# Two pools of SBUF tiles trade places: the stationary tiles of the feed-forward products move from the far end of the partition to its middle

## Chip, cores and metric

One NeuronCore of one Trainium2 chip runs the whole kernel. The metric is device time in microseconds, the median of three runs. TensorE (PE) does the matrix products, VectorE (DVE), ScalarE (ACT) and GpSimd (POOL) the rest, and SyncE (SP) issues the transfers.

## What is computed

One decoder block over 2048 positions of 1024 channels, after 16 learned positions: a normalisation, an input projection, a mixer of two head groups, an output projection with a residual, then the part that the change touches, a gated feed-forward block, and a last normalisation:

```python
n2 = rmsnorm(h, norm2_g[i])
ff = jax.nn.silu(n2 @ w_gate[i]) * (n2 @ w_up[i])      # 1024 x 2816 each
h = h + ff @ w_down[i]                                 # 2816 x 1024
out = rmsnorm(h, final_norm_g)[:, N_META:]
```

## The kernel before

**Products.** A float32 product is made of three fast matmuls (`mm3`, lines 115 to 119): each operand is split into a high part and a low remainder, and high x high, high x low, low x high are summed in PSUM. Each of the three loads a stationary operand of 128 x 128 and streams a moving operand of 128 x 512. `split` casts the high part on ACT (line 110) and takes the remainder on DVE (line 85).

**Feed-forward.** The 2048 positions are two halves `b` of 1024. Gate and up products use a seven-product scheme on 2 x 2 blocks (`seven`): the normalised rows stand as seven moving operands `X["b11"]`, `"b21"`, `"t2"`, `"t3"`, `"t1"`, `"t4"`, `"b22"`, each a high and a low tile of 8 KB per partition; the weights come in 512 KB loads (`load_raw`), are combined on POOL (`s1`, `s2`, `s4`), and are split by `part` into the rotating stationary tiles `wch` and `wcl` (ten slots each, 2 KB per partition and slot). One call of `seven` is 7 products of 12 matmuls, named `pr` in the trace; there are 44 calls. The usual order of the moving operands is b11, b21, t2, t3, t1, t4, b22; the very first call (`early`) does b11, b21, t1, b22, t2, t3, t4. The down products (`dmm`, named `pd`) do the same with the roles turned: split pieces of `ff` (`fh`, `fl`) are stationary, in the slots of `wch` and `wcl`, and the split weights are the moving tiles, in the places of b11, b21, t2 and t3 (named db11, db21, dt2, dt3).

**Where tiles lie.** A pool opened with `side="right"` is put directly below the one before it, counted from the far end of the partition (at 224 KB), and tiles within a pool go up in the order in which they are first named. From the sizes, in KB from the start of the partition:

| tiles | pool | from | to |
|---|---|---|---|
| b11, b21, b22, t1 (high and low each) | `xa`, left | 21.7 | 85.7 |
| raw loads | `xa`, left | 85.7 | 101.7 |
| t2, t3, t4 (high and low each) | `xb`, right | 102 | 150 |
| s1, s2, s4, gate and up results, u | `wc`, right | 150 | 184 |
| `wch`, then `wcl` | `wc`, right | 184 | 224 |

The output projection before it, in the trace `po`, has its own tiles in the same space, in pools that are closed when the feed-forward pools open: `wb` (160 to 224, the split weights `wh`, `wl`, moving), `mc` (154 to 160), `xu1` (138 to 154), `wraw` (130 to 138, the rows `hx` that are stored as `h2_d`), `wo` (102 to 130, with the stationary `mh`, `ml` at 104 to 120 and the scratch `jk`). The `xa` tiles begin at a multiple of 64 bytes; all tiles on the right begin 32 bytes past one.

**Order.** Instructions are put in order per engine when the program is built, by a simulated timeline, and wait for each other through semaphores. The first writer of a pool that lies over closed pools waits for the last users in those pools: in the instructions of this program the first cast into `wch` waits for the last `po` matmul, and the first cast into `xt2h` for the last two stores of `hx`, although its own place lies over `pin` and `mh` alone.

Of the kernel before, what the change touches and what calls it, by code (L numbers as in the profile page):

```python
# [10 lines left out]
F32R = mybir.dt.float32r  # L11
# [5 lines left out]
P = 128  # L17
# [20 lines left out]
def kernel(  # L38
# [68 lines left out]
    def split(hi, lo, src, scale=None, e=V):  # L107

        if scale is None:
            A.copy(hi, src)  # L110
            tt(lo, src, hi.bitcast(F32), S_, e)
        else:
            A.activation(hi, src, AF.Copy, scale=scale)
            stt(lo, src, scale, hi.bitcast(F32), M_, S_)
# [731 lines left out]
    gu = ExitStack()  # L846
# [87 lines left out]
            x_rows(0, t - 2, ("b11", "b21", "b22", "t1"))  # L934
    wo.close()
    wb_s.close()
    wc_p = gu.enter_context(tc.tile_pool(name="wc", bufs=1, side="right"))
    xb_p = gu.enter_context(tc.tile_pool(name="xb", bufs=1, side="right"))

    def load_raw(w, f):  # L940
        raw = xa_p.tile([P, KD, P], F32, name="raw", tag="raw", bufs=4)
# [1 line left out]
        return raw  # L943

    def part(src):
        hi = wc_p.tile([P, 4, P], F32R, name="wch", tag="wch", bufs=10)
        lo = wc_p.tile([P, 4, P], F32R, name="wcl", tag="wcl", bufs=10)
        split(hi, lo, src)
        return hi, lo

# [11 lines left out]
    def seven(ws, c, done, early=False):  # L962
# [3 lines left out]
        def prod(a, xn):  # L966
            o = mm_tile("pr")
            ah, al = a if isinstance(a, tuple) else part(a)
            for k in range(4):
                mm3(o, ah[:, k], al[:, k], X[xn][0][:, k], X[xn][1][:, k], k == 0, k == 3)  # L970
            return o
# [26 lines left out]
    def parts(ws):  # L998
        return [part(a) for a in ws]
# [93 lines left out]
    def f_split(g):  # L1093
        if g >= len(seq):
            return
        raw = fraw.pop(g)
        ffs[g] = []
        for q in range(NQ):
            n = min(4, NM - 4 * q)
            hi = wc_p.tile([P, 4, P], F32R, name="fh", tag="wch", bufs=10)  # L1100
            lo = wc_p.tile([P, 4, P], F32R, name="fl", tag="wcl", bufs=10)
            split(hi[:, :n], lo[:, :n], raw[:, 4 * q:4 * q + n])
            ffs[g].append((hi, lo))

# [82 lines left out]
    w_load(0, 2)  # L1187
    w_split(0, 0)
    f_split(0)
    w_split(0, 1)  # L1190
    f_split(1)
    w_split(0, 2)
    f_load(2)
    g = 0
    for g, (i, n) in enumerate(seq):
        if g == 0:
            o, o1 = mm_tile("pd"), mm_tile("pd")
            for m in range(NM + 4):
                if m < NM:
                    dmm(o, 0, m)  # L1200
                if m >= 4:
                    dmm(o1, 1, m - 4)
        elif g == 1:
            o = o1
        else:
            o = mm_tile("pd")
            for m in range(NM):
                dmm(o, g, m)
        ffs.pop(g)
        if g >= 1:  # L1210
            f_split(g + 1)
        f_load(g + 3)
        if n == 3:
            w_load(i + 1, 0)
            w_split(i + 1, 0)
        if n == 5:
            w_load(i + 1, 1)
            w_load(i + 1, 2)
        take(i, n, o)
        if n == len(pairs) - 1:  # L1220
            w_split(i + 1, 1)
            w_split(i + 1, 2)
# [32 lines left out]
```

## Time and profile before

| | |
|---|---|
| median of 3 runs | 1885.26 us (1885.22 to 1886.34) |
| profiled execution, its own time | 1885.98 us |
| span of its instructions | 1884.2 us, mean granted clock 0.988 |
| PE busy | 1822.9 us, 97% |
| DVE, ACT, POOL busy | 1232.4, 673.8, 816.9 us |
| feed-forward (`pr`), about | 578 to 1459 us |
| down products (`pd`), about | 1459 to 1877 us |

The profiled execution took 1.8 us more than its span, and 0.7 us more than the median of the runs. A matmul's recorded duration is modelled and overlaps the next one; the distance from one start to the next is what a matmul costs. Times in the rows are microseconds from the start of the span, durations of groups in nanoseconds.

### The profile page before, as it was taken

How to read it: one execution, taken by the hardware profiler on the slowest of the kernel's cores; microseconds unless marked ns; L12 is line 12 of the kernel's file. 1: busy time of each engine (PE TensorE's matmuls, PEld its weight loads, DVE VectorE, ACT ScalarE, POOL GpSimd, SP SyncE). 2: the span in 40 equal slices, each digit the busy share in tenths (PEclk: the TensorE clock that was granted, in tenths of full speed). 3: DMA queues.
4: the chain of work that ended last, by engine and by line, in shares of the span. 5: the costliest groups of instructions: out<-in, count | busy, mean ns of one | idle time of the engine just before them, and what ended most of it. 6: DMA issues, size and time to landing. Idle time of an engine off the chain costs nothing.

```text
span 1884.2 us, 23676 instructions
## 1 busy us (share of the span) xinstructions
PE 1822.9 (97%) x8497; PEld 1495.4 (79%) x8497; DVE 1232.4 (65%) x1913; ACT 673.8 (36%) x1213; POOL 816.9 (43%) x619
## 2 busy tenths in 40 slices
PE   7989997899999999999999999999999999999998
PEld 5767786788887888888887788888888888888886
DVE  6996777866457866656667866766666444445763
ACT  4333334243454333332334332333223343333441
POOL 1684425633344565453656866665662000003400
PEclk9999998999999999999999999999999999999999
DMA  6255424444355344443436554554447765536771
GB/s 182 72 176 183 144 96 145 174 168 140 112 175 167 106 157 140 140 157 107 156 117 211 194 166 151 163 179 150 133 150 228 227 198 170 154 109 208 245 218 69
DMA packets 260518, 298.37 MB, mean 158 GB/s; under 512 B 17148, under 2 KB 204048, under 8 KB 255536
## 3 DMA queue, kind: packets, MB, share of 16 engines
q1 hardware_dynamic: 260304, 296.84, 49.5%
q8 instruction: 67, 1.10, 0.2%
q14 instruction: 51, 0.42, 0.1%
q0 software_dynamic: 96, 0.01, 0.0%
HBM read 202.37 MB, written 96.53 MB: 159 GB/s over the span
## 4 chain that ended last, share of the span: by engine, by line
PE 73%; DVE 3%; DMA 2%; POOL 1%; issue 1%; ACT 1%; DVEq 0%; POOLq 0%; ACTq 0%
PE pr L117 14%; PE pr L118 14%; PE pr L119 14%; PE pd L117 8%; PE pd L118 8%; PE pd L119 8%; PE po L117 2%; PE po L119 2%; PE po L118 2%; DVE wcl L85 1%; PE pgate L774 1%; DMA hr<-h_d 1%; PE ptx L865 1%; DMA xp<-xr_d 0%; PE ppool L760 0%
## 5 line engine op out<-in xcount | busy, mean ns | idle before, releaser
L110 ACT CAST wch<-raw 128x512 fp32r<-128x512 f32 x176 | 108.7, 621 | 268.2 <-PE pr L118 240.8
L85 DVE TENSOR_TENSOR wcl<-raw,wch 128x512 fp32r<-128x512 f32 x176 | 175.7, 1001 | 37.4 <-ACT wch L110 37.0
L85 DVE TENSOR_TENSOR fl<-fr,fh 128x512 fp32r<-128x512 f32 x168 | 116.9, 707 | 126.3 <-ACT fh L110 126.2
L110 ACT CAST fh<-fr 128x512 fp32r<-128x512 f32 x168 | 96.2, 584 | 202.4 <-PE pd L118 175.0
L110 ACT CAST wch<-s 128x512 fp32r<-128x512 f32 x132 | 82.1, 622 | 224.2 <-PE pr L118 174.6
L85 POOL TENSOR_TENSOR s<-raw 128x512 f32<-128x512 f32 x44 | 67.8, 1540 | 174.7 <-DVE wcl L85 75.3
L85 DVE TENSOR_TENSOR wcl<-s,wch 128x512 fp32r<-128x512 f32 x132 | 118.3, 896 | 19.4 <-ACT wch L110 19.1
L85 POOL TENSOR_TENSOR db22h<-db22h,hd 128x512 f32<-128x512 f32 x4 | 5.2, 1292 | 256.2 <-DVE db22h L85 256.2
L117 PE MATMUL pj<-wh,xh 128*128 128x512 f32 x256 | 102.6, 409 | 2.6 <-ACT xh L110 2.3
L117 PE MATMUL po<-wh,mh 128*128 128x512 f32 x256 | 103.8, 406 | 0.7 <-ACT mh L110 0.7
L119 PE MATMUL pj<-wh,xl 128*128 128x512 f32 x256 | 103.0, 407 | 0.0
L118 PE MATMUL pj<-wl,xh 128*128 128x512 f32 x256 | 102.7, 403 | 0.0
L119 PE MATMUL po<-wh,ml 128*128 128x512 f32 x256 | 100.4, 393 | 0.8 <-DVE ml L85 0.8
L118 PE MATMUL po<-wl,mh 128*128 128x512 f32 x256 | 100.7, 393 | 0.0
L85 POOL TENSOR_TENSOR rs<-rv,mhalf 128x1 f32<-128x1 f32 (+2 forms) x35 | 31.5, 900 | 154.1 <-DVE rv L91 144.8
L85 POOL TENSOR_TENSOR wr<-wr 128x512 f32<-128x512 f32 x44 | 66.8, 1519 | 72.4 <-DMA wr<-in_w_down_dram 64.5
L85 DVE TENSOR_TENSOR gt<-gt,ut 128x512 f32<-128x512 f32 x88 | 92.9, 1057 | 0.0
L85 POOL TENSOR_TENSOR tmp<-z,pk 64x512 f32<-64x512 f32 x32 | 50.8, 1588 | 79.8 <-issue 64.7
L85 DVE TENSOR_TENSOR gt<-pr,gt 128x512 f32<-128x512 f32 x66 | 45.5, 690 | 60.3 <-PE pr L119 60.1
L85 POOL TENSOR_TENSOR ut<-gt 128x512 f32<-128x512 f32 x22 | 33.6, 1528 | 107.2 <-DVE gt L85 107.2
L117 PE MATMUL pr<-xt2h,wch 128*128 128x512 f32 x176 | 70.5, 400 | 5.3 <-DVE gt L85 3.6
L1006 ACT ACTIVATE gt<-gt 128x512 f32<-128x512 f32 x88 | 55.6, 633 | 50.8 <-DVE gt L85 50.8
(392 smaller groups left out, 5586.1 us busy)
## 6 DMA issues: line engine op xcount, KB each, us to landing
fr<-ff_d SPq DMA_DIRECT2D x56, 704.0 KB, 4.9
raw<-in_w_gate_dram SPq DMA_DIRECT2D x44, 512.0 KB, 4.8
raw<-in_w_up_dram SPq DMA_DIRECT2D x44, 512.0 KB, 4.3
ff_d<-gt SPq DMA_DIRECT2D x22, 1024.0 KB, 3.9
pk<-pk_d SPq DMA_DIRECT2D x16, 1284.0 KB, 6.2
ff_d<-ut SPq DMA_DIRECT2D x22, 768.0 KB, 5.6
wr<-in_w_down_dram SPq DMA_DIRECT2D x22, 512.0 KB, 3.3
wd_d<-wr SPq DMA_DIRECT2D x22, 512.0 KB, 3.4
```

The costliest lines, as they stand in the source:

```text
L85: e.tensor_tensor(o, a, b, op=op)
L110: A.copy(hi, src)
L117: PE.matmul(o, lh, rh, start=first, stop=False)
L118: PE.matmul(o, lh, rl, start=False, stop=False)
L119: PE.matmul(o, ll, rh, start=False, stop=last)
L774: PE.matmul(pg[:, k * P:(k + 1) * P], glubd[:, k], gt[:, k], start=True, stop=True)
L865: PE.transpose(pt[:, k], r[:, (4 * h + k) * P:(4 * h + k + 1) * P], ident)
L1006: lambda i, j: A.activation(gt[:, i, j], gt[:, i, j], AF.Silu), b == 0 and f0 == 0)
```

## The change

The pool `xb` (t2, t3, t4 and their namesakes of the down products) is opened first and so lies at the far end. The pool `wc` follows, without the rotating stationary tiles, and these have a pool `wk` of their own, opened last. The number of slots and the order of all calls stay.

```diff
     wo.close()
     wb_s.close()
+    xb_p = gu.enter_context(tc.tile_pool(name="xb", bufs=1, side="right"))
     wc_p = gu.enter_context(tc.tile_pool(name="wc", bufs=1, side="right"))
-    xb_p = gu.enter_context(tc.tile_pool(name="xb", bufs=1, side="right"))
+    wk_p = gu.enter_context(tc.tile_pool(name="wk", bufs=10, side="right"))
...
     def part(src):
-        hi = wc_p.tile([P, 4, P], F32R, name="wch", tag="wch", bufs=10)
-        lo = wc_p.tile([P, 4, P], F32R, name="wcl", tag="wcl", bufs=10)
+        hi = wk_p.tile([P, 4, P], F32R, name="wch", tag="wch")
+        lo = wk_p.tile([P, 4, P], F32R, name="wcl", tag="wcl")
...
-            hi = wc_p.tile([P, 4, P], F32R, name="fh", tag="wch", bufs=10)
-            lo = wc_p.tile([P, 4, P], F32R, name="fl", tag="wcl", bufs=10)
+            hi = wk_p.tile([P, 4, P], F32R, name="fh", tag="wch")
+            lo = wk_p.tile([P, 4, P], F32R, name="fl", tag="wcl")
```

From the sizes, the places after it: `wch` at 102 to 122 KB, `wcl` at 122 to 142, the rest of `wc` at 142 to 176, t2, t3 and t4 at 176 to 224. The `xa` tiles stay. Every shift is a multiple of 2 KB.

## Rows read from the trace of the kernel before

**Rows 1.** Busy time by stretch: stretch, length, PE, PEld, DVE, ACT, POOL, clock, DMA.
```profile
650.00:1000.00 350.00, 350.00 (x1551) 285.43 (x1550) 231.28 (x296) 117.87 (x198) 184.34 (x125) 1.00 0.44 141
1060.00:1450.00 390.00, 390.00 (x1689) 317.00 (x1688) 269.90 (x330) 125.45 (x203) 236.21 (x155) 1.00 0.52 164
1470.00:1870.00 400.00, 400.00 (x1737) 325.85 (x1736) 208.40 (x308) 143.02 (x256) 43.36 (x38) 1.00 0.59 180
```
**Rows 2.** Waits of PE from 600 to 1880 us: total us, times, longest.
```profile
PE pr L117 <- DVE gt L85: 4.1, 3, 2.2
```
**Rows 3.** Groups of PE by form: out<-moving,stationary, count, busy us, mean ns.
```profile
L117 PE MATMUL pr<-xb21h,wch 128*128 128x512 f32 x176 | 69.7, 396 | 0.0
L117 PE MATMUL pr<-xt3h,wch 128*128 128x512 f32 x176 | 68.6, 390 | 0.0
...
L117 PE MATMUL pr<-xt4h,wch 128*128 128x512 f32 x176 | 69.0, 392 | 0.4 <-DVE gt L85 0.4
L117 PE MATMUL pd<-db11h,fh 128*128 128x512 f32 x176 | 69.7, 396 | 0.0
...
L117 PE MATMUL pd<-db21h,fh 128*128 128x512 f32 x144 | 57.0, 396 | 0.0
L117 PE MATMUL pd<-dt3h,fh 128*128 128x512 f32 x152 | 59.2, 390 | 0.0
L117 PE MATMUL pd<-dt2h,fh 128*128 128x512 f32 x144 | 56.3, 391 | 0.0
```
**Rows 4.** Timeline of PE, the first matmul of four successive products.
```profile
802.86 0.40 PE L117 MATMUL pr<-xb21h,wch 128*128 128x512 f32 x1
...
805.66 0.39 PE L117 MATMUL pr<-xt2h,wch 128*128 128x512 f32 x1
...
808.40 0.39 PE L117 MATMUL pr<-xt3h,wch 128*128 128x512 f32 x1
...
811.12 0.40 PE L117 MATMUL pr<-xt1h,wch 128*128 128x512 f32 x1
```
**Rows 5.** Timeline of PE, output projection: first and last of eleven matmuls in a row.
```profile
450.95 0.39 PE L117 MATMUL po<-wh,mh 128*128 128x512 f32 x1
...
453.22 0.39 PE L118 MATMUL po<-wl,mh 128*128 128x512 f32 x1
```
**Rows 6.** Timeline of ACT at the start of the feed-forward part.
```profile
577.24 1.14 ACT L110 CAST wch<-raw 128x512 fp32r<-128x512 f32 x2 [1.16 <-PE po L119]
...
580.84 0.62 ACT L110 CAST xt2h<-xp 128x512 fp32r<-128x512 f32 x1 [1.32 <-DMA h_d<-hx]
...
591.38 0.61 ACT L110 CAST xt3h<-xp 128x512 fp32r<-128x512 f32 x1
```
**Rows 7.** Timeline of PE in the same stretch, first matmuls of products and the last `po`.
```profile
576.81 0.39 PE L119 MATMUL po<-wh,ml 128*128 128x512 f32 x1
577.91 0.50 PE L117 MATMUL pr<-xb11h,wch 128*128 128x512 f32 x1 [0.71 <-ACT wch L110]
...
591.52 0.50 PE L117 MATMUL pr<-xt2h,wch 128*128 128x512 f32 x1 [1.36 <-ACT xt2h L110]
...
599.16 0.39 PE L117 MATMUL pr<-xt4h,wch 128*128 128x512 f32 x1
```
**Rows 8.** Tile hx from 574 to 582 us: its last store, its landing time, its waiter.
```profile
L817 SPq DMA_DIRECT2D h_d<-hx x1: 320/320/320, 578.0 to 578.0; - x1
...
  ACT xt2h L110: 1.3, 1
...
DMA to landing us min/median/max: 2.7/2.7/2.7
```
**Rows 9.** Timeline of DVE, the same stretch.
```profile
592.28 0.68 DVE L85 TENSOR_TENSOR xt3l<-xp,xt3h 128x512 fp32r<-128x512 f32 x1
```
**Rows 10.** Busy time by stretch, columns as in rows 1: gaps of PE and the clock.
```profile
209.80:213.60 3.80, 0.47 (x3) 0.03 (x1) 3.71 (x8) 1.21 (x3) 2.99 (x2) 1.00 0.39 103
...
214.40:217.80 3.40, 3.40 (x14) 2.92 (x13) 3.31 (x10) 0.59 (x1) 0.86 (x1) 0.51 0.00 0
...
593.40:596.80 3.40, 3.40 (x9) 2.63 (x9) 1.53 (x4) 1.18 (x2) 0.00 (x0) 0.50 0.92 266
```

## The prediction

> **What bounds the kernel now.** I first looked where PE is idle, since the change touches only PE's operands. In three long stretches, 1140 us in all, PE is busy for the whole length, at full clock, with DVE at 52 to 69% and the others lower [rows 1]; from 600 us to the end PE waits only 4.1 us for others [rows 2]. So from 600 us on the time is a number of matmuls times the distance from one start to the next. That distance is not one number. In steady state the products on b21 take (805.66 - 802.86) / 12 = 233.3 ns each, those on t3 (811.12 - 808.40) / 12 = 226.7 ns, those on t2, which come after a slow product, (808.40 - 805.66) / 12 = 228.3 ns [rows 4]. The groups say the same in their modelled durations: 396 ns with a moving operand in b11 or b21 (t1 and b22 alike), in the down products too, 390 to 392 ns with one in t2, t3 or t4 [rows 3]. The slow ones are the tiles at 22 to 86 KB, the fast ones those on the right. So place, or something that goes with it, does cost time on this chip, 6.7 ns or 2.9% of a matmul, and the change is about place. The question is whose place.
>
> **Part 1, the rate of the products.** The change moves the stationary tiles from 184-224 KB to 102-142, and t2, t3, t4 from 102-150 to 176-224. The slow moving tiles stay at 22-86.
>
> For t2, t3, t4 the trace has nearly the new pair already: in the output projection the moving `wh`, `wl` lie at 160-224 and the stationary `mh`, `ml` at 104-120, and eleven matmuls in a row give (453.22 - 450.95) / 10 = 227 ns [rows 5]. That is the fast value, so I put nothing on these.
>
> For the slow tiles the new pair (moving at 22-86, stationary at 102-142) stands nowhere in the trace. The bounds: at best each comes down to 226.7 ns, at worst it stays at 233.3; worse than that no row shows for a matmul in steady state. Their number: b11, b21, t1, b22, three matmuls each, are 12 groups of 176 [one in rows 3], 2112; db11 is three groups of 176 and db21 three of 144 [rows 3], 960; together 3072. Times 6.67 ns that is 20.5 us. With no slow product ahead of them t2 and t4 (2 x 528 matmuls) would also lose their 1.67 ns, another 1.8 us. So part 1 is worth between 0 and -22.3 us.
>
> I take 0. The stationary tile's place leaves no mark in the trace: `wch` lies at 184-204 and `wcl` at 204-224, and the three matmuls of a triple, two with the one and one with the other, take the same; stationary at 184-224 with t3 and stationary at 104-120 with `wh` give the same 227 ns [rows 4, 5]. The nearness of the two isn't it either: t1 ends at 86 KB, 98 below the nearest stationary tile, and is slow; t2 begins at 102 KB, up to 122 below the farthest, and is fast once settled. What does sort the rows is the moving tile alone, by its place (below 86 or above 102 KB) or by its start: the `xa` tiles start at a multiple of 64 bytes, everything on the right, stationary tiles too, 32 bytes past one. The change leaves both as they are, since the `xa` tiles stay and every shift is a multiple of 2 KB.
>
> A rule to weigh here: the Trainium skill (TensorE: Matmul & The Clock Gate, Part 2: What happens when you issue a matmul) has the next tile's weights read through a port of their own, which takes no bandwidth from the running matmul. By that rule the stationary tiles' place can't matter, and part 1 is 0 as well. The trace agrees that their place leaves no mark, but not that place is without effect: the page has no reason for 233.3 against 226.7 ns.
>
> **Part 2, the start of the feed-forward part.** Here a wait changes hands. Now `wc` lies over `wb`, `mc` and `xu1`, and its first cast goes as soon as the last `po` is done, at 577.24 us; PE starts `pr` at 577.91 [rows 6, 7]. `xb` lies over `wo`, `wraw` and part of `xu1`, and its first cast, `xt2h`, waits for the last store of `hx`, issued at 578.0, landed 2.7 us later, and starts at 580.84 [rows 6, 8]. After the change `wk` lies over `wo`, `wraw` and `xu1`, so the first cast into `wch` inherits that wait, while `xb` lies over `wb` alone and is free at 577.2. `s1`, `s2`, `s4` stay over `mc`, `wb` and `xu1` and keep their start.
>
> The first `pr` moves from 577.91 to 580.84 + (577.91 - 577.24) = 581.51, 3.6 us later. Behind the waiting cast ACT has its other casts, and if the built order leaves those of `xt2h` and `xt3h` behind it, they wait too; DVE's remainders follow either way, and the SP queue holds only loads that wait for these casts. PE is then without work for 4.7 us from 576.81. A gap of 3.8 us was followed by 3.4 us at half clock (0.51, which is 1.2 GHz) [rows 10], so I add 1.7 us for that.
>
> Against this stands a stall that the kernel already has. PE now reaches t2 early, waits, starts at 591.52 [rows 7], gets its pieces one by one until DVE's last `xt3l` at 592.28 + 0.68 = 592.96 [rows 9], and then runs 3.4 us at half clock [rows 10]; it begins t4 only at 599.16 [rows 7]. After the change the four products before t2 take 48 x 0.2333 = 11.2 us, plus 0.45 us that they lose on the first remainders, plus 1.7 for the clock: t2 starts at 581.51 + 13.35 = 594.9, when its pieces are there if they come no more than 1.9 us later than now. Then t2 and t3 take 24 x 0.228 = 5.5 us and t4 starts at 600.3, 1.2 us later than now. Without the half clock it would be 0.5 us earlier; without the cover it is rival 2. So part 2 costs +1.2 us, between -0.5 and +5.3.
>
> **The sum.** 1885.98 us is the profiled execution, 0.7 over the median; 1.8 of it lie around the span and don't change. 1885.98 + 0 + 1.2 = 1887.2 for that execution, 1886.5 against the median of 1885.26. Within 0.2% (3.8 us), about what a measurement of this kernel tells from no change, it is the same.
>
> **Rival 1, the stationary tile matters after all.** It may matter for low moving tiles only, where no row can show it: then 233.3 falls to 226.7 ns at best, and the time is 1886.5 - 22.3 = 1864.2, or something between. For it: the one placement like the new one, the output projection, is fast [rows 5], and the slow tiles are those that never met a stationary tile in the middle. Against it: nothing else in the rows moves with the stationary place. DVE has room for 1.2% more speed [rows 1].
>
> **Rival 2, the later start isn't covered.** The casts of the t2 and t3 pieces stand behind the waiting cast on ACT, and their loads behind them, so the pieces come 3.6 + 1.7 us later, as PE does, and the old stall is met again. Then the whole delay stays: 1885.3 + 5.3 = 1890.6. It decides from the point where the last `xt3l` ends later than about 594.9 us, now 592.96. For it: the casts at 591.38 come after a silu that needs PE's second product [rows 6]. Against it: with `xb` free at once, ACT can cast the first pieces while it has nothing else.
>
> **Rival 3, the fast tiles become slow.** If t2, t3, t4 at the far end fall to 233.3 ns, 9 x 176 + 3 x 152 + 3 x 144 = 2472 matmuls [one of each in rows 3] pay 6.67 ns, 16.5 us, less the 1.8 already paid: 1886.5 + 14.7 = 1901.2. Against it stand the rows of `po` [rows 5], in which only stationary places up to 120 KB occur.
>
> **How the numbers follow.** Forecast (rate unchanged, start covered): 0.60, 1886.5 us, on its own 1884 to 1889. Rival 1: 0.22. Rival 2: 0.13. Rival 3: 0.05. Faster by over 0.2% is rival 1, 0.22; within 0.2% is the forecast, 0.60; slower is rivals 2 and 3, 0.18. Rival 1 is too likely to be left out, so the range reaches to it and to rival 2: 1863 to 1891; rival 3 stays outside.
>
> **What would show it.** Right: in steady state 233.3 ns between starts on b11 and b21, 226.7 on t3; the first `wch` cast released by the store of `hx` at about 580.8; the first `pr` near 581.5; a stretch at half clock after it; t2 without a wait; t4 at about 600. Wrong: groups of `pr` on b11 or b21 below 396 ns (rival 1, then the down products on db11 too), t3 above 390 (rival 3), or a wait of PE for `xt2h` beyond 595 us (rival 2). That the build shifts other orders by some us is the rest of the risk.

## The result and the profile after

| | before | after |
|---|---|---|
| median | 1885.24 us, 4 runs (1883.08 to 1886.34) | 1898.42 us, 4 runs (1896.79 to 1899.44) |
| profiled execution, its own time | 1885.98 us | 1898.18 us |
| span, mean granted clock | 1884.2 us, 0.988 | 1896.4 us, 0.984 |

The changed kernel is slower: ratio 1.0071, interval 1.0053 to 1.0088. In a later series with more runs it was 1.0055, interval 1.0041 to 1.0069 (below, the changed kernel again). The forecast was 1886.5 us in a range of 1863 to 1891, so the time lies outside it, on the side that had a chance of 0.18.

**The rate of the products did not change.** The changed kernel's groups of PE by form (out<-moving,stationary, count, busy us, mean ns):

```profile
L117 PE MATMUL pr<-xb21h,wch 128*128 128x512 f32 x176 | 69.8, 397 | 0.0
L117 PE MATMUL pd<-db11h,fh 128*128 128x512 f32 x176 | 69.7, 396 | 0.0
L117 PE MATMUL pr<-xt4h,wch 128*128 128x512 f32 x176 | 69.1, 392 | 0.8 <-DVE gt L85 0.4 <-ACT wch L110 0.3
L117 PE MATMUL pr<-xt3h,wch 128*128 128x512 f32 x176 | 68.5, 389 | 0.0
```

These are the values of [rows 3] to 1 ns. The timeline of PE, first matmuls of four successive products, gives the distances:

```profile
816.27 0.40 PE L117 MATMUL pr<-xb21h,wch 128*128 128x512 f32 x1
...
819.07 0.39 PE L117 MATMUL pr<-xt2h,wch 128*128 128x512 f32 x1
...
821.82 0.39 PE L117 MATMUL pr<-xt3h,wch 128*128 128x512 f32 x1
...
824.54 0.40 PE L117 MATMUL pr<-xt1h,wch 128*128 128x512 f32 x1
```

b21 takes (819.07 - 816.27) / 12 = 233.3 ns from start to start, t2 229.2 (228.3 there), t3 226.7, as in [rows 4]; 0.01 us over twelve matmuls is 0.8 ns. In the long stretches PE is as full as in [rows 1], at full clock (stretch, length, PE, PEld, DVE, ACT, POOL, clock, DMA):

```profile
655.00:1005.00 350.00, 350.00 (x1550) 285.29 (x1549) 227.60 (x291) 117.97 (x199) 181.62 (x123) 1.00 0.42 135
...
1480.00:1880.00 400.00, 400.00 (x1737) 325.87 (x1736) 209.28 (x310) 144.38 (x259) 43.27 (x38) 1.00 0.60 182
```

**The time went at the start of the feed-forward part.** The timelines of ACT, PE and DVE there (start, length, operation, idle time before it and what ended it):

```profile
581.52 0.62 ACT L110 CAST xt2h<-xp 128x512 fp32r<-128x512 f32 x1 [1.16 <-PE po L119]
...
585.66 1.14 ACT L110 CAST wch<-raw 128x512 fp32r<-128x512 f32 x2 [1.34 <-DMA h_d<-hx]
```
```profile
581.10 0.39 PE L119 MATMUL po<-wh,ml 128*128 128x512 f32 x1
586.33 0.79 PE L117 MATMUL pr<-xb11h,wch 128*128 128x512 f32 x1 [4.85 <-ACT wch L110]
...
589.39 0.80 PE L119 MATMUL pr<-xb11h,wcl 128*128 128x512 f32 x1 [0.98 <-DVE wcl L85]
...
602.06 0.40 PE L117 MATMUL pr<-xt2h,wch 128*128 128x512 f32 x1
...
608.00 0.47 PE L117 MATMUL pr<-xt4h,wch 128*128 128x512 f32 x1 [0.34 <-ACT wch L110]
...
614.26 0.47 PE L117 MATMUL pr<-xb11h,wch 128*128 128x512 f32 x1 [3.25 <-DVE gt L85]
```
```profile
582.19 1.19 DVE L85 TENSOR_TENSOR xt2l<-xp,xt2h 128x512 fp32r<-128x512 f32 x1
...
586.66 1.77 DVE L85 TENSOR_TENSOR xt3l<-xp,xt3h 128x512 fp32r<-128x512 f32 x1
...
588.64 1.30 DVE L85 TENSOR_TENSOR wcl<-raw,wch 128x512 fp32r<-128x512 f32 x2
```

The releasers of [rows 6] have changed hands: `xt2h` now goes behind the last `po`, the first `wch` behind the store of `hx`. The wait of PE behind `po` has grown from 1.10 to 5.24 us between starts. And there are two things that the prediction didn't have: DVE takes four remainders of t2 and t3, 6.2 us of work, before the first `wcl`, and PE waits 3.25 us at the start of the second call of `seven`, for a `gt` of DVE (the operation that adds a finished product to the gate results).

The store itself (tile `hx`, its last store, its waiter, its landing time; before: [rows 8]):

```profile
L817 SPq DMA_DIRECT2D h_d<-hx x1: 320/320/320, 582.3 to 582.3; - x1
...
  ACT wch L110: 1.3, 1
...
DMA to landing us min/median/max: 3.3/3.3/3.3
```

The clock, by stretch, columns as in the stretches above:

```profile
584.30:594.50 10.20, 7.18 (x16) 5.25 (x17) 10.17 (x15) 6.66 (x13) 5.63 (x4) 0.50 0.54 159
...
615.00:618.40 3.40, 3.40 (x9) 2.64 (x8) 3.18 (x6) 1.26 (x2) 1.33 (x1) 0.50 0.27 71
```

The half clock (0.50, which is 1.2 GHz) begins in the gap, at 584.3 us, and holds for 10.2 us, three times the 3.4 of [rows 10].

**Where the time went, by sections.** From the starts of single matmuls in the two traces, in us. The first and second `seven` are the first two calls; the ends of a section are the starts that the headings name.

| section | before | after | difference |
|---|---|---|---|
| last `po` to first `pr` | 1.10 | 5.24 | +4.14 |
| first `pr` to first on t4 | 21.26 | 21.67 | +0.41 |
| first on t4 to second `seven` | 2.72 | 6.25 | +3.53 |
| second `seven` | 19.42 | 21.02 | +1.60 |
| the rest of `pr` | 829.25 | 827.48 | -1.77 |
| `pd` | 425.87 | 425.87 | 0 |
| last `po` to last `pd` | 1299.6 | 1307.5 | +7.9 |

The two spans differ by 12.2 us. The other 4.3 lie ahead of the last `po`, which stands at 581.10 instead of 576.81 us, though up to there both kernels have the same instructions in the same order. In the changed kernel again the last `po` stood at 578.89, and over the kernels below between 573.3 and 582.2. Of the 4.3 us, 2.3 arise at one place: behind a wait of PE that both have, the profile after shows half clock and the profile before doesn't (clock by stretch, before and then after):

```profile
546.70:550.10 3.40, 3.40 (x16) 2.77 (x15) 1.37 (x5) 0.69 (x3) 2.23 (x3) 1.00 0.23 88
```
```profile
546.70:550.10 3.40, 3.40 (x12) 3.11 (x13) 1.45 (x2) 2.51 (x7) 2.55 (x2) 0.50 0.14 53
```

Nine of the ten profiles below, also those of kernels with the order of before, have such a stretch between 528 and 551 us. I count these 4.3 us to the execution and not to the change, and read every kernel below by its time from last `po` to last `pd`.

Single sections scatter in the same way. The half clock at 593 us [rows 10] is missing in four of the kernels below that have the order and the wait of before (the new pool in the order of before, four different starts, only the stationary tiles shifted, fine starts); they go from the first `pr` to t4 in 19.6 to 19.7 us instead of 21.26. So differences of up to 2 us in a single section can be the execution's; over the whole way the first of these four, whose products take the same times, came to 1300.0 us, against 1299.6.

### The profile page after: what moved, and what is told of

Read it like the earlier page. It is cut to its first block, busy times and chain, and to the rows that moved or that the text cites. A ratio compares the mean times of both kernels' runs of the same rounds, so it can differ in the third digit from the quotient of the medians.

```text
span 1896.4 us, 23680 instructions
## 1 busy us (share of the span) xinstructions
PE 1828.5 (96%) x8497; PEld 1501.1 (79%) x8497; DVE 1232.0 (65%) x1913; ACT 674.9 (36%) x1213; POOL 815.6 (43%) x619
## 4 chain that ended last, share of the span: by engine, by line
PE 73%; DVE 3%; DMA 2%; issue 1%; POOL 1%; ACT 1%; POOLq 0%; DVEq 0%; SPq 0%; ACTq 0%
PE pr L117 14%; PE pr L118 14%; PE pr L119 14%; PE pd L117 8%; PE pd L118 7%; PE pd L119 7%; PE po L117 2%; PE po L119 2%; PE po L118 2%; DVE wcl L85 1%; PE pgate L774 1%; DMA hr<-h_d 1%; POOL s L85 1%; PE ptx L865 1%; DMA raw<-in_w_gate_dram 0%
## 5 line engine op out<-in xcount | busy, mean ns | idle before, releaser
L117 PE MATMUL pr<-xb11h,wch 128*128 128x512 f32 x176 | 71.9, 409 | 8.1 <-ACT wch L110 4.8
L85 DVE TENSOR_TENSOR gt<-pr,u 128x512 f32<-128x512 f32 x66 | 45.3, 687 | 45.7 <-PE pr L119 42.3
```

The costliest lines, as they stand in the source:

```text
L85: e.tensor_tensor(o, a, b, op=op)
L117: PE.matmul(o, lh, rh, start=first, stop=False)
```

## The experiments

Times are medians beside runs of the kernel before on the same chip; the ratio comes with its interval from the comparison run by run and need not be the quotient of the medians; "from `po` to `pd`" is the last row of the table above, 1299.6 us before and 1307.5 after.

### The new places with the old wait

The pool of `hx` is opened first and so lies at 216 to 224 KB, under t4. The feed-forward tiles keep the places of the changed kernel.

```diff
     vt_p = mid.enter_context(tc.tile_pool(name="vt", bufs=1))
+    raw_p = wb_s.enter_context(tc.tile_pool(name="wraw", bufs=2, side="right"))
     wb_p = wb_s.enter_context(tc.tile_pool(name="wb", bufs=1, side="right"))
...
-    raw_p = wb_s.enter_context(tc.tile_pool(name="wraw", bufs=2, side="right"))
```

> The changed kernel, with one line moved: the pool of the rows hx (wraw) is opened first, at 216 to 224 KB, so that the new pool of the stationary tiles lies over wo and xu1 and no longer over hx; t2, t3, t4 lie over it instead, as before the change. All feed-forward tiles keep the places of the changed kernel. Theory A (the loss is the wait for the last store of hx that the first wch cast inherits, with what follows from it: idle PE, half clock, another order): the first wch cast waits only for the last po and one square on ACT (about 1.4 us), PE's gap before the first pr falls from 5.2 us to about 2.5, and the time comes back to 1885 to 1889 us. Theory B (the places themselves slow something down): the time stays near 1898 us.

Measured: 1890.61 us against 1887.62 (10 and 19 runs), ratio 1.0008, interval 0.9998 to 1.0017; from `po` to `pd` 1300.1 us, 0.5 more than before. The first `wch` no longer waits for the store (timelines of ACT and PE):

```profile
582.82 1.14 ACT L110 CAST wch<-raw 128x512 fp32r<-128x512 f32 x2
```
```profile
583.49 0.50 PE L117 MATMUL pr<-xb11h,wch 128*128 128x512 f32 x1 [2.35 <-ACT wch L110]
```

PE's gap is 2.74 us between starts (ACT does a `jk` first, built ahead of the cast). The time is above the 1885 to 1889 us expected, on a chip on which the kernel before, too, is 2.4 us slower than in the first series. What follows: with the tiles at their new places the loss is gone. The places as such cost nothing that this comparison could tell.

### The old places with the new wait

The same line moved in the kernel before, so that `wc`, with the stationary tiles at 184 to 224 KB as before, lies over `hx`.

```diff
     vt_p = mid.enter_context(tc.tile_pool(name="vt", bufs=1))
+    raw_p = wb_s.enter_context(tc.tile_pool(name="wraw", bufs=2, side="right"))
     wb_p = wb_s.enter_context(tc.tile_pool(name="wb", bufs=1, side="right"))
...
-    raw_p = wb_s.enter_context(tc.tile_pool(name="wraw", bufs=2, side="right"))
```

> The kernel before, with the same one line moved: the feed-forward tiles stay where they were, but wc (stationary tiles, s1, s2, s4) now lies over hx and has to wait for its last store, while t2, t3, t4 don't. Theory A (the wait): the time goes up by 8 to 14 us, to 1893 to 1899 us, with a gap of about 5 us before the first pr and a stretch at half clock after it. Theory B (the places): it stays at 1885 us.

Measured: 1895.42 us against 1887.62 (4 and 19 runs), ratio 1.0038, interval 1.0023 to 1.0053; from `po` to `pd` 1306.9 us, 7.3 more than before. Timeline of PE, and the clock by stretch:

```profile
582.20 0.80 PE L117 MATMUL pr<-xb11h,wch 128*128 128x512 f32 x1 [4.43 <-ACT wch L110]
```
```profile
580.10:590.30 10.20, 6.96 (x16) 4.98 (x17) 10.20 (x10) 7.33 (x14) 7.75 (x5) 0.50 0.41 127
```

The gap is 4.82 us, the half clock again 10.2 us, and at the start of the second `seven` PE waits again (2.84 us more than before in that section, where the changed kernel has 3.53). What follows: the wait makes the loss without any tile of the feed-forward part having moved. The two experiments together show that the loss goes with the wait and not with the places; how it divides among the order on DVE, the half clock and the second `seven` they don't show.

### The new pool, opened in the order of before

In the changed kernel `wc` and `wk` are opened ahead of `xb`: t2, t3, t4 at 102 to 150 KB as before, the stationary tiles at 150 to 190, the rest of `wc` at 190 to 224.

```diff
-    xb_p = gu.enter_context(tc.tile_pool(name="xb", bufs=1, side="right"))
     wc_p = gu.enter_context(tc.tile_pool(name="wc", bufs=1, side="right"))
     wk_p = gu.enter_context(tc.tile_pool(name="wk", bufs=10, side="right"))
+    xb_p = gu.enter_context(tc.tile_pool(name="xb", bufs=1, side="right"))
```

> The changed kernel with the pool of the stationary tiles opened ahead of that of t2, t3, t4: stationary tiles at 150 to 190 KB, t2, t3, t4 at 102 to 150 as before, the rest of wc at 190 to 224. The pool of its own is kept, the wait is the old one (first wch cast after the last po, first xt2h after the store of hx). Theory A: 1885 us within 2 us. Theory B: if the pool of its own or the stationary tiles' place costs, 1890 us or more. In either, 233.3 and 226.7 ns between starts as before.

Measured: 1888.25 us against 1887.62 (10 and 19 runs), ratio 1.0003, interval 0.9992 to 1.0014; from `po` to `pd` 1300.0 us; PE's gap 1.10 us as before, and the distances 233.3 and 226.7 ns as before. The 1885 us expected went by the first series; beside the kernel before on this chip the difference is 0.6. What follows: neither the pool of its own nor a third place of the stationary tiles matters.

### The moving tiles on the left, 32 bytes further

The prediction had left open whether the slow products are sorted by the place of the moving tile or by its start. In the kernel before, a small constant ahead of them is made 32 bytes longer, so that b11, b21, b22 and t1 start, as the stationary tiles do, 32 bytes past a multiple of 64.

```diff
-    halfb = const.tile([P, 4], F32, name="halfb")
+    halfb = const.tile([P, 12], F32, name="halfb")[:, :4]
```

> The kernel before, with one small constant tile 32 bytes larger, so that every tile of the left side after it, b11, b21, b22 and t1 among them, starts 32 bytes later, at 32 past a multiple of 64 bytes as the tiles on the right do. The order of all instructions is the same. If the 233.3 ns go with the start modulo 64 bytes: products on b11, b21, t1, b22 come down to 226.7 ns and the time to about 1863 us. If they go with the place below 86 KB: 233.3 ns and 1885 us.

Measured: 1869.07 us against 1887.62 (4 and 19 runs), ratio 0.9897, interval 0.9881 to 0.9914; from `po` to `pd` 1278.8 us, 20.8 less than before. All products are fast, by form:

```profile
L117 PE MATMUL pr<-xb21h,wch 128*128 128x512 f32 x176 | 68.5, 389 | 0.0
...
L117 PE MATMUL pd<-db11h,fh 128*128 128x512 f32 x176 | 68.5, 389 | 0.0
```

and b11 takes 226.7 ns from start to start:

```profile
841.88 0.39 PE L117 MATMUL pr<-xb11h,wch 128*128 128x512 f32 x1
...
844.60 0.39 PE L117 MATMUL pr<-xb21h,wch 128*128 128x512 f32 x1
```

What follows: it is the start and not the place. The 20.8 us are near the 22.3 that the prediction had worked out as the most that the slow tiles could give; the medians differ by 18.6, and the 1863 us expected were not reached. This kernel is faster than the kernel before and the changed one.

### Only the stationary tiles shifted

Does the start of the moving tile count by itself, or against that of the stationary tile? In the kernel before, 32 bytes are added at the end of two pools. The stationary tiles then start at a multiple of 64 bytes, as b11, b21, b22, t1 do; t2, t3, t4 stay 32 bytes past one.

```diff
...
+    def end_pad(pool):
+        if pool not in padded:
+            padded.add(pool)
+            pool.tile([P, 8], F32, name="pad32", tag="pad32")
...
         lo = wc_p.tile([P, 4, P], F32R, name="wcl", tag="wcl", bufs=10)
+        end_pad(wc_p)
...
             x_tile(xb_p if nm in ("t2", "t3", "t4") else xa_p, nm)
+            if nm == "t4":
+                end_pad(xb_p)
```

> The kernel before, with 32 bytes of padding past the stationary tiles and past t4: the stationary tiles now start at a multiple of 64 bytes like b11, b21, b22 and t1, and t2, t3, t4 stay at 32 past one. If what counts is moving against stationary start: products on b11, b21, b22, t1 fall to 226.7 ns and those on t2, t3, t4 rise to 233.3, and the time is near 1880 us. If the moving start alone counts: 233.3 and 226.7 as before, 1885 us.

Measured: 1885.45 us in one run, 1887.69 before; from `po` to `pd` 1296.1 us. Fast and slow have changed sides, by form:

```profile
L117 PE MATMUL pr<-xt3h,wch 128*128 128x512 f32 x176 | 69.9, 397 | 0.0
...
L117 PE MATMUL pr<-xb21h,wch 128*128 128x512 f32 x176 | 68.6, 390 | 0.3 <-DVE ut L85 0.3
```

and from start to start b11 takes (845.43 - 842.71) / 12 = 226.7 ns, t2 (850.95 - 848.15) / 12 = 233.3:

```profile
842.71 0.39 PE L117 MATMUL pr<-xb11h,wch 128*128 128x512 f32 x1
...
845.43 0.39 PE L117 MATMUL pr<-xb21h,wch 128*128 128x512 f32 x1
...
848.15 0.40 PE L117 MATMUL pr<-xt2h,wch 128*128 128x512 f32 x1
...
850.95 0.40 PE L117 MATMUL pr<-xt3h,wch 128*128 128x512 f32 x1
```

The 1880 us expected were not reached: from `po` to `pd` it is 3.5 us less than before, near the 600 x 6.67 ns = 4.0 us by which 3072 fast and 2472 slow matmuls differ from the reverse. What follows: the moving tiles have not moved against a multiple of 64, and yet their rates change. What counts is the distance between the two starts. Shown as well: the stationary tile does matter, by its start, though not by its place.

### Four different starts

The left tiles as in the kernel 32 bytes further, and in addition three of them 32 bytes longer. Past a multiple of 128 bytes b11 then starts at 96, b21 at 0, b22 at 32, t1 at 64; the stationary tiles and t2, t3, t4 at 96.

```diff
...
+    def xt_(pool, nm, q, dt, pre):
+        n = 2056 if q == "l" and nm in ("b11", "b21", "b22") else 2048
+        t = pool.tile([P, n], dt, name=f"{pre}{nm}{q}", tag=f"x{nm}{q}")
+        return t[:, :2048].rearrange("p (k c) -> p k c", k=4)
...
```

> The kernel before, with the left tiles set apart by 32 bytes each, so that their starts, modulo 128 bytes, are 96 (b11), 0 (b21), 32 (b22) and 64 (t1); stationary tiles and t2, t3, t4 stay at 96. If what counts is the start modulo 64 bytes: 226.7 ns between starts on b11 and b22, 233.3 on b21 and t1. If it is modulo 128: 226.7 on b11 alone. If only the one start of before (64) was bad: 233.3 on t1 alone. Time: near 1877 us in the first case, 12 or 13 us above the kernel with all starts shifted where only b11 is fast.

Measured: 1885.71 us in one run; from `po` to `pd` 1296.4 us. In the down products db11 (start equal) is fast and db21 (32 off) slow:

```profile
L117 PE MATMUL pd<-db11h,fh 128*128 128x512 f32 x176 | 68.5, 389 | 0.0
...
L117 PE MATMUL pd<-db21h,fh 128*128 128x512 f32 x144 | 57.1, 396 | 0.0
```

In `pr` the products with start equal (b11) and 64 off (b22) each come behind one with another start. All twelve of their distances average 230 to 231 ns; b21 and t1, 32 off, take 233.5 to 235. Within the twelve the two differ: the last two on b11 take 227 ns, while b22, from its fourth on, repeats 232, 226 and 229 ns and stays at (842.84 - 840.78) / 9 = 228.9 (timeline of PE):

```profile
840.78 0.39 PE L117 MATMUL pr<-xb22h,wch 128*128 128x512 f32 x1
...
842.84 0.40 PE L117 MATMUL pr<-xb11h,wch 128*128 128x512 f32 x1
```

What follows: 64 bytes off is better than 32, but in this one kernel not as good as equal, so the effect doesn't go by the start modulo 64 alone. Each change of the relation between two products costs a run-in of several matmuls, also from b22 to b11, so that tiles that are right by turns bring little, and the 1877 us expected were not reached. Of the 3.2 us less than before, 1.6 are the half clock at 593 us [rows 10], which this execution doesn't have.

### Fine starts

The left tiles 32 bytes further, but b11 16 and b21 4 bytes beyond that.

```diff
...
+    def xt_(pool, nm, q, dt, pre):
+        a = {"b11": 4, "b21": 1}.get(nm, 0)
+        t = pool.tile([P, 2064 if a else 2048], dt, name=f"{pre}{nm}{q}", tag=f"x{nm}{q}")
+        return t[:, a:a + 2048].rearrange("p (k c) -> p k c", k=4)
...
```

> The kernel with all left starts shifted by 32 bytes, but b11 16 bytes and b21 4 bytes further still (48 and 36 past a multiple of 64), b22 and t1 at 32 as the stationary tiles. It asks how fine the effect is. If any difference of starts modulo 64 costs: 233.3 ns or another slow value on b11 and b21. If lines of 16 bytes count: b21 slow or the same, b11 between. If only 32 bytes matter: 226.7 ns on all.

Measured: 1880.56 us in one run; from `po` to `pd` 1289.8 us. Timeline of PE, first matmuls of products:

```profile
842.47 0.39 PE L117 MATMUL pr<-xb11h,wch 128*128 128x512 f32 x1
...
845.23 0.40 PE L117 MATMUL pr<-xb21h,wch 128*128 128x512 f32 x1
...
848.06 0.39 PE L117 MATMUL pr<-xt2h,wch 128*128 128x512 f32 x1
...
850.78 0.39 PE L117 MATMUL pr<-xt3h,wch 128*128 128x512 f32 x1
```

16 off: (845.23 - 842.47) / 12 = 230.0 ns. 4 off: 235.8 ns, the slowest of all. Equal (t2): 226.7 ns, right after the slow one. What follows: nearness doesn't help; of the distances tried, only equal starts give 226.7 ns.

### The changed kernel again

The changed kernel without an edit, beside eleven runs of the kernel before on one chip.

> The changed kernel once more, timed against the kernel before on this chip. In its first profile 7.9 of 12.2 us came after the last po, 4.3 before it, where both kernels have the same instructions in the same order. Theory A (the change costs only what follows the last po, the rest is the scatter of the stretch before): +6 to +10 us against before, and the last po in the new profile anywhere from 576.8 to 582.2 us, where it stood in the six profiles so far. If the part before the last po belongs to the change: +12 to +14 us and the last po near 581 us again.

Measured: 1897.47 us (1895.04 to 1900.26, 6 runs) against 1887.69 (1882.93 to 1891.34), ratio 1.0055, interval 1.0041 to 1.0069; from `po` to `pd` 1308.1 us; gap 5.34 us, half clock 10.2 us behind it. All sections of the table came out within 0.5 us of the first profile. What follows: the 7.9 us belong to the change and repeat; the place of the last `po` does not.

### The gap filled with work

In the changed kernel 27 matmuls of b11 on itself, into a PSUM tile that nobody reads, are put behind the output projection; 20 of them fall into PE's gap.

```diff
+    fill = s_tile("fill")
+    xf = X["b11"][0]
+    for i in range(27):
+        PE.matmul(fill, xf[:, i % 4, :P], xf[:, i % 4], start=i == 0, stop=i == 26)
     wo.close()
```

> The changed kernel with 27 more matmuls of 128 x 128 by 128 x 512, the high piece of b11 on itself, into a PSUM tile that nobody reads: some 7 stand between the last po matmuls and some 20 behind the last of them, in the 5.2 us in which TensorE waits for the store of hx. The waits, the casts and every other order stay those of the changed kernel. It tells how much of the loss is half clock and how much is work that comes late. From the last po to the last pd the changed kernel took 1307.5 and 1308.1 us, the kernel before 1299.6. Theory A, the gap itself sets off the half clock of 10.2 us: with TensorE at work in the gap the clock stays at full and 4 to 5 us come back, last po to last pd 1303 to 1304 us, the time 1893 us. Theory B, the half clock of 10.2 us comes from the many short waits for the late remainders that follow the gap: then it stays, or moves by a few us, and the time stays at 1897 to 1899 us, 1.5 us more if the seven added matmuls between the po delay these. In both the first pr stands 5 us behind the last po, since the store of hx sets it.

Measured: 1890.27 us against 1884.10 (10 and 19 runs), ratio 1.0031, interval 1.0015 to 1.0048; from `po` to `pd` 1301.9 us, 5.6 less than the changed kernel. The gap is full, the first `pr` as far behind the last `po` as in the changed kernel (5.24 us). Timeline of PE, then the clock by stretch:

```profile
580.80 4.72 PE L938 MATMUL fill<-xb11h 128*128 128x512 f32 x20
585.81 0.50 PE L117 MATMUL pr<-xb11h,wch 128*128 128x512 f32 x1 [0.29 <-ACT wch L110]
...
588.94 0.50 PE L119 MATMUL pr<-xb11h,wcl 128*128 128x512 f32 x1 [1.88 <-DVE wcl L85]
```
```profile
584.30:589.50 5.20, 3.03 (x12) 1.76 (x11) 5.17 (x8) 3.01 (x6) 4.29 (x3) 1.00 0.44 119
589.60:593.00 3.40, 3.40 (x10) 2.62 (x9) 3.40 (x6) 3.12 (x7) 0.79 (x1) 0.50 0.75 227
```

The sum is near theory A's, a little below it, and the clock did what A says: full behind the gap, 3.4 us at half instead of 10.2, and that behind the wait for the first `wcl`. But the gain doesn't sit where A has it. Up to t4 it is only 21.67 - 20.49 = 1.2 us, since the late `wcl` holds PE up at either clock. Another 3.5 come from the wait at the second `seven`, which is gone, and 1.6 from the second `seven` itself. In this kernel the build put the `gt` in question elsewhere on DVE, ahead of the remainders behind which it stands in the changed kernel (timelines of DVE, this kernel and the changed one):

```profile
606.50 0.69 DVE L85 TENSOR_TENSOR gt<-pr,u 128x512 f32<-128x512 f32 x1 [0.34 <-PE pr L119]
```
```profile
613.43 0.68 DVE L85 TENSOR_TENSOR gt<-pr,u 128x512 f32<-128x512 f32 x1
```

So two things changed at once here, and how much of the 5.6 us the clock alone gives is not settled beyond the 1.2 us of the first section.

### The changed kernel with the shift

The changed kernel with the same one-line shift of 32 bytes on the left.

```diff
-    halfb = const.tile([P, 4], F32, name="halfb")
+    halfb = const.tile([P, 12], F32, name="halfb")[:, :4]
```

> The changed kernel, with all tiles of the left side 32 bytes further out, as in e4, so that every moving tile begins at the same distance from a multiple of 64 bytes as the stationary tiles. It tells whether the rate of the products and the late start are independent. If they are, it gains on the changed kernel what e4 gained on the kernel before: last po to last pd falls by 20.8 us from 1307.5 to 1308.1, to 1287 us, all products 226.7 ns from start to start, and the time is 1878 us, 9 us slower than e4. Rival: with the stationary tiles in the middle of the partition the slow value has another cause and products on b11 and b21 stay at 233.3 ns, 1897 us.

Measured: 1871.63 us against 1884.10 (10 and 19 runs), ratio 0.9948, interval 0.9934 to 0.9963; from `po` to `pd` 1286.2 us, 21.3 less than the changed kernel and 7.4 more than the kernel before with the shift. The products on b21 are fast here too:

```profile
L117 PE MATMUL pr<-xb21h,wch 128*128 128x512 f32 x176 | 68.8, 391 | 0.0
```

What follows: the late start and the rate of the products are independent, and add. The gain of the shift is the same with the stationary tiles in the middle. The median is 6 us below what was expected; on this chip the kernel before, too, is 3.5 us below the chip of the shift alone, and in the profiled execution the last `po` stands at 573.3 us, the earliest of all.

## Why the prediction was wrong

**Part 1, right.** The rate was put at no change, and it is none: 233.3 and 226.7 ns in the same products, so rivals 1 and 3 fall. The reason was half right. That the place leaves no mark holds for two more placements, 102 to 142 KB and 150 to 190. That "what does sort the rows is the moving tile alone" does not: with only the stationary tiles shifted by 32 bytes the slow and the fast products change sides. The change left the relation of the starts as it was, every shift being a multiple of 2 KB, so the sum came out. The alternative that the text named, place or start, was settled for the start, and what rival 1 priced at 22.3 us at most is there, but not for this change to take.

The rule weighed there, of the Trainium skill (TensorE: Matmul & The Clock Gate, Part 2: What happens when you issue a matmul), that the next weights come through a read port of their own and take nothing from the running matmul, gave the right answer for the change. It has no room for the shift of the stationary tiles alone, by which the same products take 226.7 instead of 233.3 ns. What ties the two operands' starts together no run shows.

**Part 2, right in the wait that changes hands, wrong in what follows from it.** The wait did change hands as described: first `wch` released by the store of `hx`, `xt2h` free behind the last `po`, a stretch of half clock behind the gap, t2 without a wait. Forecast were +1.2 us; from `po` to `pd` it was +7.9. By its terms:

- *First `pr`:* +3.6 forecast, +4.1 measured. The store took 3.3 us to land instead of 2.7.
- *First `pr` to t4:* 5.5 + 13.35 = 18.8 us forecast, 21.7 measured. This is the cover, which was to give back 2.4 us and gave none (before: 21.26). The half clock was sized by a gap of 3.8 us that was followed by a run of matmuls without a break [rows 10]. Here it lasted 10.2 us, of which PE was busy 7.18, so by estimate it cost half of that, 3.6, instead of 1.7. The wait for the first remainders, put at 0.45 as before, was then about 15.73 - 11.2 - 3.6 = 0.9, with 15.73 from first `pr` to t2 (PE's own row has 0.98). Behind t3 another 0.5 went. The stall to be covered was itself sized by one execution: without the half clock at 593 us, as in four kernels above, t4 comes 1.6 us earlier.
- *The second `seven`:* nothing forecast. PE came 3.5 us late to its start, waiting for a `gt` that stands on DVE behind the remainders, and 1.6 more went in it, with half clock behind that wait.
- *The rest:* nothing forecast, -1.8 measured. Before, 3.4 us at half clock stand at 1047 us, at the change of halves; in the changed kernel there are none, in either of its two profiles; the fine starts, with the order of before, have none either, so this need not be the change's. The same stretch before and after:

```profile
1047.30:1050.70 3.40, 3.40 (x10) 2.65 (x9) 2.99 (x5) 2.14 (x4) 0.00 (x0) 0.50 1.03 283
```
```profile
1047.30:1050.70 3.40, 3.40 (x17) 2.74 (x16) 2.71 (x5) 0.00 (x0) 3.40 (x3) 1.00 0.82 334
```

The differences, 0.5 + 2.9 + 3.5 + 1.6 - 1.8, make the 6.7 us between 1.2 and 7.9. The step that failed is the one on DVE. "DVE's remainders follow either way" was true, but in which order was not asked, and so the second `seven` was put at nothing. The larger part, 3.5 + 1.6, is that `gt`, built on DVE behind the remainders of the next products; in the kernel with the gap filled, where the clock differs as well, it stands ahead of them, and both losses are gone. At the start, with `xb` free first, four remainders of t2 and t3 went ahead of the first `wcl`, which PE needs next and which now came 3.0 us behind its `wch` (585.66 to 588.64 us) where it had come 0.7 behind. The other term that was mis-sized is the half clock, 3.6 by estimate where 1.7 stood. No run separates the late `wcl` from the longer half clock. The sentence on the SP queue and ACT looked at what is behind the waiting instruction; what PE then waited for came late by what went ahead of it.

**Rival 2** had the result, a start that isn't covered, at 5.3 us, but by another way: pieces of t2 and t3 that come too late. They came first, and were never waited for. Its price was too low since it left out the remainders and the second `seven`.

**The range** ended at 1891. With the 7.9 us the sum is 1893.2; the medians are 4 to 5 us more. Of these 4.3 lie, in the profiled execution, ahead of the last `po`, in instructions that the change doesn't touch, and in the second series the difference of the medians, 9.8 us, is near the 8.5 from `po` to `pd`. Why the half clock at 547 us comes in one execution and not in another was not tried. A range for one median should have held some us for it.

## What to carry to other kernels

Whoever moves a pool moves the waits of its first writers, so look up for each engine not only what is queued behind the new wait but what will be built ahead of it, DVE's small operations above all. Don't price the half clock behind a gap by one other gap: 3.4 us of it stood behind a gap of 3.8 us and unbroken work, 10.2 behind one of 5.2 and broken work, and which of the two differences made it longer was not separated. And look at the start addresses of the two operands of a matmul before their places: 32 bytes on one side were worth 18.6 us of 1888 to the kernel, while moving 88 KB of tiles by tens of KB changed no product.

## What was not expected of the hardware

- The distance between matmuls of 128 x 128 by 128 x 512, each with a weight load, depends on the start of the moving tile against that of the stationary tile: 226.7 ns when they are equal modulo 128 bytes, 230.0 at 16 bytes off, 233.3 at 32, 235.8 at 4, and 229 at 64 off, the last in one kernel alone. Why is open. Equal and 32 off were seen with the stationary tiles in three places of the partition.
- Behind a product with another relation a fast one can need some matmuls to settle: t2 behind b21 takes 228.3 and 229.2 ns in the rows above, on the mean of twelve, t3 behind t2 226.7. Behind the slow b21 at 4 bytes off, t2 was fast at once.
- The stretch at half clock after a gap was 10.2 us in all four profiles in which PE was idle for 4.8 to 5.3 us at this place (the changed kernel twice, the old places with the new wait, the changed kernel with the shift), 6.8 us behind the gap of 2.74 us of the new places with the old wait, and 3.4 us where the gap was filled with work, after a wait of 1.9. The wait alone doesn't decide: at 544 us PE waited 2.1 us in the kernel before, with full clock behind it.
- PE's fastest value here is 226.7 ns. The Trainium skill (TensorE: Matmul & The Clock Gate, Back-to-back issue gap) gives about 216 ns between starts for isolated matmuls of 512 columns and about 131 ns in a sustained stream; no run here shows either.
